# Hybrid streaming-encoder block: value, key and query columns regrouped into a 264-column and a 512-column projection

## Chip, cores and metric

The kernel runs on one core of one Trainium2 chip. The metric is device time in microseconds (us) of one execution; less is better. The kernel before has a median of 1688.1 us over three runs (1687.12 to 1690.24).

## What is computed

The reference is one layer on x of 1024 tokens by 1024 channels, with a memory of 256 tokens. Cut to what matters:

```python
h = _rmsnorm(x, norm_mix_g)
z = h @ w_in                       # one input projection, f32
hq, hf, hi, hg, fq, fk, fv, ff, mq, gate_logits = split(z)
y_a = _hgrn2_mixer(hq, hf, hi, hg, ...)              # gated linear recurrence
y_b = _fox_mixer(fq, fk, fv, ff, fox_f_bias, ...)    # forgetting attention
y_c = _memory_mixer(mq, rmsnorm(mem) @ mem_kv_w, ...)  # attention into 256 memory tokens
merged = sum(gate_i * (y_i @ w_br_i)); x = x + merged @ w_out
x = x + conv_glu_ffn(_rmsnorm(x, norm_ffn_g), ...)

# in _fox_mixer (8 heads of 64 channels):
log_f = log_sigmoid(f_logit + f_bias); Fc = cumsum(log_f)
s = q_norm . k_norm * scale + Fc[t] - Fc[s]; p = softmax(causal s); o = p @ v
```

The change concerns the projections of the forgetting attention (called fox in the code): `fv`, 512 value columns; `ff`, 8 forget logits, one per head; and `fk`, `fq`, keys and queries, of which the kernel projects one pair of heads (256 columns: 128 of keys, 128 of queries) before the attention begins.

## The kernel before

**Products.** Every f32 product is done as three matmuls of fp32r parts (`mm3`, L246 to L250): high by high (L248), high by low (L249), low by high (L250). The parts are made by `split` (L260): a cast to fp32r on ACT gives the high part (L254), a subtraction on DVE gives the low part (L262). K = 1024 is eight chunks of 128.

**Weights of this stage.** `weights` (L276) loads a piece of weights (two K-chunks of 512 columns or four of 256 or 264) with a DMA on SP's queue (L273) into `raw` (two buffers), and splits it into `wh` and `wl` (four buffers each, `WIDE`).

**The projection.** `token_major` (L793) loads all pieces of a block of columns and then goes over eight token blocks of 128: for each it takes a PSUM tile from `ps_proj` (named `pp` in the trace, three buffers), issues 8 x 3 = 24 matmuls with the normalised tokens (`uh`, `ul`, 128 x 128) as the stationary operand and the weights as the moving one, and calls `evac`, which copies the tile out and so frees its buffer for the block three later.

**The three passes.** `fox_values` (L823) calls it twice: value columns 0 to 255 (256 columns wide, evacuated by one ACT copy, L827), and value columns 256 to 511 with the 8 forget columns (264 wide, the ACT copy and a DVE operation, L829, that scales the forget logits and adds the bias `fbr` into `ffx`). Then come log-sigmoid and cumulative sum of the forget logits. `fox_proj` (L967) calls it for the first pair's keys and queries (256 wide, ACT copy into `z`, L973), and after every fourth block normalises z (L979 to L982).

**What is woven in.** `weave` (L98, called in L1331) alternates these projections with `memory` (cross-attention into the memory tokens): `mem_prep` loads one head's queries (`mqf`, L868), squares them on ACT (`msq`, L873), sums the squares with one-column matmuls on PE (L876) into a `tr` tile, and splits them into `mqh` and `mql`; `mem_parts` loads and splits the memory's keys and values (`mkv`, L858; `mkh` and `mvh` on POOL, the low parts on DVE); `mem_attn` does logits, softmax, transposes (L912) and the product with the values. The memory part is given a higher priority by `ahead`; a scheduler then turns the emitted program into one order of instructions per engine, and each engine runs its own order in sequence, waiting on semaphores. A wait thus holds back all that stands behind it on its engine.

**SP's queue at this place.** The bias `fbr` (4 KB, L818), the first `mqf` and the first `mkv` (512 KB each) are issued on SP one behind the other, between two weight loads.

**Afterwards** comes the attention proper with the second pair's projections, in an order set by a planner; its products of fox projections are recorded at L1229.

Of the kernel before, what the change touches and what calls it, by code (L numbers as in the profile page):

```python
# [197 lines left out]
def tile_block(ctx: ExitStack, tc: tile.TileContext, xT, memT, x_rows, mem_rows, vec, fbias, mats, hmask, w_first, w_cm, w_late, w_fqk, w_fv,  # L198
# [594 lines left out]
    def token_major(src, ncol, evac, lead=False):  # L793

        with tc.issue_after(late["load"].ins):
            per = 2 if ncol == HB else 4
            w = [weights(src[q], (per, ncol)) for q in range(KC // per)]
        if lead:
            yield
        for tb in range(8):  # L800
            ps = ps_proj()[:, :ncol]
            tsl = slice(tb * P, (tb + 1) * P)
            for k in range(KC):
                wh, wl = w[k // per]
                mm3(ps, uh[k][:, tsl], ul[k][:, tsl], wh[:, k % per, :], wl[:, k % per, :], k == 0, k == KC - 1)
            evac(tb, ps)
            yield
# [14 lines left out]
    negFd = tc.dram_tile([8, T], F32, name="negFd")  # L822

    def fox_values():
        for pc in range(2):
            def evac(tb, ps, pc=pc):
                S.activation(Vf[:, tb, pc * 256:(pc + 1) * 256], ps[:, :256], AF.Copy, scale=rt[:, tb:tb + 1])  # L827
                if pc:
                    V.scalar_tensor_tensor(out=ffx[:, tb, :], in0=ps[:, 256:264], scalar=rt[:, tb:tb + 1], in1=fbr,  # L829
                                           op0=ALU.mult, op1=ALU.add)  # L830
            yield from token_major(w_fv[pc], 264 if pc else 256, evac)

        S.activation(ffe, ffx, AF.Abs)
        S.activation(ffe, ffe, AF.Sigmoid)
        S.activation(ffe, ffe, AF.Ln)
        V.scalar_tensor_tensor(out=ffe, in0=ffx, scalar=0.0, in1=ffe, op0=ALU.min, op1=ALU.add)
        for n in range(2):
            pt = ps_tr()
            for b in range(4):
                PE.transpose(pt[:8, b * P:(b + 1) * P], ffe[:, 4 * n + b, :], ident)  # L840
            V.tensor_tensor_scan(negF[:, n * HB:(n + 1) * HB], ones[:8, 0:1].to_broadcast([8, HB]), pt[:8, :],
                                 0.0 if n == 0 else negF[:, HB - 1:HB], ALU.mult, ALU.subtract)
        SP.dma_start(negFd, negF)
        yield
# [79 lines left out]
    def memory():  # L924
        run_all(mem_prep(0))
        mem_parts()
        yield
        for h in range(4):
            if h < 3:
                run_all(mem_prep(h + 1))  # L930
            yield from mem_attn(h)
# [35 lines left out]
    def fox_proj():  # L967

        def evac(tb, ps):
            n, b = tb // 4, tb % 4  # L970
            if b == 0:
                fox_tile(0, n)
            S.activation(fox_z[0, n][:, b, :], ps, AF.Copy, scale=rt[:, tb:tb + 1])  # L973
            if b == 3:
                z = fox_z[0, n].rearrange("p b (h d) -> p (b h) d", d=64)
                r = cp.tile([P, 16], F32, tag="fr", name="fr", bufs=2)
                for i in range(2):
                    sq = gate_tile().rearrange("p (h d) -> p h d", d=64)
                    S.activation(sq, z[:, 8 * i:8 * i + 8, :], AF.Square)  # L979
                    V.reduce_sum(r[:, 8 * i:8 * i + 8], sq, axis=AX.X)  # L980
                rstd_small(r, r, 64)
                V.tensor_mul(z, z, r.unsqueeze(2).to_broadcast([P, 16, 64]))  # L982

        yield from token_major(w_fqk[0], 256, evac)

    qk, qk_ready, vh, vh_ready, nfs, nf_ready = {}, {}, {}, {}, {}, {}
    pt_ready, pt_free, rows_done, turn, kept = {}, {}, {-1: 0.0, -2: 0.0}, {}, {}
# [340 lines left out]
            yield "SP", 0.1, max(t, vh_ready[7])  # L1328
            SP.dma_start(Vf[:, tb, :], hid[tb])

    weave((chain(fox_values(), fox_proj()), 25), (ahead(memory(), AHEAD), 4 * MEM_STEPS))  # L1331
    parts[-1] = [(weights(w_fqk[1][q], (4, 256)), q, 0.0) for q in range(2)]
    pm.release()
    pf = pools["pf"] = Rounded(tc, name="pf", bufs=1, side="right", reuse_waits="tile")
    pf.small(("st", 4, 4))
# [760 lines left out]
def _layout(inp):  # L2096
    import numpy as np

    f = {k: np.asarray(v, dtype=np.float32) if np.asarray(v).dtype != np.float32 else np.asarray(v)
         for k, v in inp.items()}  # L2100
    c = np.ascontiguousarray

    def kmaj(a):

        return a.reshape(a.shape[0] // P, P, a.shape[1]).transpose(1, 0, 2)

    def chunks(a):

        k, n = a.shape
        return c(a.reshape(k // P, P, n // P, P).transpose(2, 1, 0, 3).reshape(n // P, P, k))  # L2110

    def cols(v):
        return v.reshape(-1, P).T

    x, mem = f["x"][0], f["mem"][0]
    w = f["w_in"][0]
    hq, hf, hi, hg, fq, fk, fv, ff, mq, gt = np.split(
        w, np.cumsum([512, 512, 512, 512, 512, 512, 512, 8, 512]), axis=1)
    o = {}
# [13 lines left out]
    o["fbias"] = c(np.broadcast_to(f["fox_f_bias"][0][None, :], (P, 8)))  # L2133
    i = np.arange(P)
    o["mats"] = c(np.concatenate([
        (i[:, None] == i[None, :]).astype(np.float32), np.ones((P, P), np.float32),
        np.where(i[:, None] >= i[None, :], 0.0, NEG).astype(np.float32),
        np.broadcast_to((np.arange(HB) % P != 0).astype(np.float32)[None, :], (P, HB))], axis=1))
    hm = []
    for H in (16, 8):  # L2140
        t = i.reshape(-1, 2, H)[:, 1, :].reshape(-1)
        hm.append(i[:, None] // H == (t // H - 1)[None, :])
    hm.append((i[:, None] // 8 == i[None, :] // 8) & (i[:, None] <= i[None, :]))
    o["hmask"] = c(np.concatenate(hm, axis=1).astype(np.float32))
    cm = np.concatenate([hq, hf, hg, mq, gt], axis=1)
    o["w_cm"] = chunks(cm)
    first = np.stack([o["w_cm"][16 + 8 * br + j].reshape(P, KC, P) for br, j in ORDER[:2]], axis=2)
    o["w_first"] = c(first.reshape(P, 2, 2 * KC * P // 2).transpose(1, 0, 2))

    def quartered(a):  # L2150

        q = kmaj(a).reshape(P, 2, 4, 2, P).transpose(0, 1, 3, 2, 4)
        return np.stack([q[:, h, c].reshape(P, -1) for h, c in ((0, 0), (0, 1), (1, 1), (1, 0))], axis=1)

    o["w_pair"] = c(np.stack([quartered(np.concatenate([cm[:, ch * P:(ch + 1) * P] for ch in pair], axis=1))
                              for pair in PAIRS]))

    def pieces(a, cuts):
        out = []
        for lo, hi_ in cuts:  # L2160
            p = kmaj(a[:, lo:hi_])
            out.append(np.stack([p[:, 0:4].reshape(P, -1), p[:, 4:8].reshape(P, -1)]))
        return out

    o["w_fqk"] = c(np.stack([pieces(np.concatenate([fk[:, p * P:(p + 1) * P], fq[:, p * P:(p + 1) * P]], axis=1),
                                    [(0, 256)])[0] for p in range(2)]))
    late = np.concatenate([m[:, p * P:(p + 1) * P] for p in (2, 3) for m in (fk, fq)], axis=1)
    o["w_late"] = c(np.stack([kmaj(m).reshape(P, 4, 2 * HB).transpose(1, 0, 2) for m in (late, hi)]))
    pv = pieces(np.concatenate([fv, ff], axis=1), [(0, 256), (256, 520)])
    o["w_fv0"], o["w_fv1"] = c(pv[0]), c(pv[1])  # L2170
    kv = f["mem_kv_w"][0]
    half = lambda m: kmaj(m).reshape(P, 4, 2 * HB).transpose(1, 0, 2)
    o["w_mkv"] = c(np.concatenate([half(kv[:, :512]), half(kv[:, 512:])]))
    o["w_br"] = c(np.stack([chunks(f[n][0]) for n in ("w_br_hgrn", "w_br_fox", "w_br_mem")]))
    o["w_out"] = chunks(f["w_out"][0])

    up = kmaj(f["ffn_w_up"][0]).reshape(P, 2, 4, 2, NF // 2, 2, P).transpose(4, 3, 0, 1, 5, 2, 6)
    up = np.stack([up[..., 0, 0, :, :], up[..., 0, 1, :, :], up[..., 1, 1, :, :], up[..., 1, 0, :, :]], axis=3)
    o["w_up"] = c(up.reshape(NF, P, 4, HB))

    wd = f["ffn_w_down"][0].reshape(NF // 2, 2, P, 2, HB).transpose(2, 3, 1, 0, 4)
    o["w_dn"] = c(wd.reshape(P, 4, NF // 2, HB))
    return o
# [19 lines left out]
```

## Time and profile before

| | us |
|---|---|
| Median of three runs (lowest, highest) | 1688.1 (1687.12, 1690.24) |
| The profiled execution's own time | 1688.31 |
| Its span, first to last instruction | 1686.5 |
| Around the span | 1.8 |
| TensorE (PE) busy | 1677.7 (99%), 8409 matmuls |
| VectorE (DVE), ScalarE (ACT), GpSimd (POOL) busy | 1170.4, 808.5, 326.6 |
| Mean granted TensorE clock | 1.000 of full speed |

All times of the trace are microseconds from the start of the span. A row of the timeline gives start, duration, engine, line, operation, output and inputs, the count, and in brackets how long the engine was idle before and what released it. "PEld" is the load of the stationary operand, which lies beside matmuls. The stage of the change begins at 258 us (first matmul of the first value block) and ends at 371 us (last block of the first pair's keys and queries). A matmul's own duration includes its way through the array (0.28 us at 256 columns), so what one costs in a stream is the distance between starts (0.12 us).

### The profile page before, as it was taken

The page shows a single profiled execution, that of the slowest core. Times are in us where ns is not written, and L with a number is a line of the kernel's source. Part 1 is how long each engine was busy: PE and PEld are TensorE (multiplying, and loading weights), DVE is VectorE, ACT ScalarE, POOL GpSimd, SP SyncE. Part 2 cuts the span into 40 slices and gives each one's busy share as a digit, 9 for nine tenths or more (in the row PEclk, how much of TensorE's full clock was granted, in tenths as well). Part 3 has the DMA queues.
Part 4 walks back from the last instruction along what each step waited for, and adds up shares of the span by engine and source line. Part 5 has one row for each costly group of instructions (what it writes and reads, how often), then busy time and mean ns, then how long its engine had stood idle before and what let it go on. Part 6 is the DMA issues. An engine that isn't in the chain of part 4 may idle for free.

```text
span 1686.5 us, 23254 instructions
## 1 busy us (share of the span) xinstructions
PE 1677.7 (99%) x8409; PEld 1415.8 (84%) x8409; DVE 1170.4 (69%) x2118; ACT 808.5 (48%) x1459; POOL 326.6 (19%) x430
## 2 busy tenths in 40 slices
PE   9999999999999999999999999999999999999999
PEld 7888889998888888888888888888888888888887
DVE  6966554558688766766856745988788888775664
ACT  6734444656576556666521333634344444533432
POOL 0200001336464423433201000211111111100000
PEclk9999999999999999999999999999999999999999
DMA  9442324122142233100337641666454454494782
GB/s 376 171 145 105 118 77 157 71 100 69 57 133 87 75 101 101 51 20 19 107 106 257 207 151 58 189 180 182 132 144 131 122 166 132 176 352 154 239 283 88
DMA packets 87348, 235.50 MB, mean 140 GB/s; under 512 B 9904, under 2 KB 12600, under 8 KB 87104
## 3 DMA queue, kind: packets, MB, share of 16 engines
q1 hardware_dynamic: 68032, 166.83, 28.4%
q0 software_dynamic: 18624, 66.59, 13.9%
q8 instruction: 66, 1.08, 0.3%
q10 hardware_dynamic: 576, 0.59, 0.1%
q14 instruction: 50, 0.41, 0.1%
HBM read 184.91 MB, written 72.13 MB: 152 GB/s over the span
## 4 chain that ended last, share of the span: by engine, by line
PE 96%; DVE 2%; ACT 1%; DMA 1%; issue 0%; ACTq 0%; DVEq 0%
PE pp L250 17%; PE pp L249 17%; PE pp L248 17%; PE pp L1229 10%; PE lg L248 5%; PE lg L250 5%; PE lg L249 5%; PE tr L250 3%; PE tr L249 3%; PE tr L248 3%; PE tr L1147 2%; PE po L1172 1%; PE lg L1085 1%; PE lg L1086 1%; PE po L248 1%; PE po L249 1%
## 5 line engine op out<-in xcount | busy, mean ns | idle before, releaser
L254 ACT CAST wh<-s 128x512 fp32r<-128x512 f32 x122 | 73.3, 620 | 133.1 <-PE pp L249 73.3
L254 ACT CAST wh<-rw 128x512 fp32r<-128x512 f32 x96 | 58.5, 619 | 113.8 <-PE pp L249 69.7
L254 ACT CAST wh<-raw 128x512 fp32r<-128x512 f32 (+2 forms) x85 | 63.9, 756 | 96.0 <-PE pp L249 76.3
L254 ACT CAST dwh<-wr 128x1024 fp32r<-128x1024 f32 (+1 forms) x41 | 40.2, 980 | 114.1 <-PE tr L249 37.6
L250 PE MATMUL pp<-uh,wl 128*128 128x512 f32 x224 | 89.0, 397 | 0.0
L248 PE MATMUL pp<-uh,wh 128*128 128x512 f32 x224 | 88.8, 396 | 0.0
L249 PE MATMUL pp<-ul,wh 128*128 128x512 f32 x224 | 88.4, 395 | 0.0
L1161 DVE TENSOR_TENSOR pl<-tr,ph 128x512 fp32r<-128x512 f32 (+1 forms) x96 | 51.4, 551 | 30.7 <-ACT ph L254 30.3
L1120 ACT ACTIVATE pt<-pt,st 128x128 f32<-128x128 f32 (+3 forms) x64 | 49.6, 775 | 45.9 <-DVE st L1116 30.6
L1229 PE MATMUL pp<-wl,uh 128*128 128x512 f32 (+1 forms) x192 | 70.0, 365 | 0.0
L1229 PE MATMUL pp<-wh,uh 128*128 128x512 f32 (+1 forms) x192 | 69.5, 362 | 0.0
L1229 PE MATMUL pp<-wh,ul 128*128 128x512 f32 (+1 forms) x192 | 69.4, 362 | 0.0
L262 DVE TENSOR_TENSOR dwl<-wr,dwh 128x1024 fp32r<-128x1024 f32 (+1 forms) x41 | 46.3, 1130 | 30.5 <-ACT dwh L254 30.5
L254 ACT CAST ph<-tr 128x512 fp32r<-128x512 f32 (+1 forms) x96 | 44.2, 477 | 41.0 <-PE tr L1147 39.6
L1124 POOL TENSOR_SCALAR pt<-pt,st 128x128 f32<-128x128 f32 (+3 forms) x64 | 52.0, 815 | 60.1 <-DVE st L1122 58.4
L1828 POOL DMA_DIRECT2D rw<-in_w_up x42 | 23.2, 558 | 200.0 <-DVE wl L1718 190.1
L1718 DVE TENSOR_TENSOR wl<-rw,wh 128x512 fp32r<-128x512 f32 x69 | 46.6, 687 | 21.2 <-PE pp L250 17.9
L1718 DVE TENSOR_TENSOR wl<-s,wh 128x512 fp32r<-128x512 f32 x85 | 57.9, 683 | 0.0
L262 DVE TENSOR_TENSOR wl<-raw,wh 128x512 fp32r<-128x512 f32 (+2 forms) x54 | 52.1, 964 | 7.0 <-ACT wh L254 7.0
L248 PE MATMUL pp<-wh,uh 128*128 128x256 f32 (+1 forms) x192 | 55.2, 287 | 0.0
L250 PE MATMUL pp<-wh,ul 128*128 128x256 f32 (+1 forms) x192 | 55.0, 286 | 0.0
L249 PE MATMUL pp<-wl,uh 128*128 128x256 f32 (+1 forms) x192 | 54.4, 283 | 0.0
(520 smaller groups left out, 5602.2 us busy)
## 6 DMA issues: line engine op xcount, KB each, us to landing
rw<-in_w_up POOLq DMA_DIRECT2D x42, 512.0 KB, 4.8
sd<-in_w_dn POOLq DMA_DIRECT2D x30, 512.0 KB, 6.0
br<-yd SPq DMA_DIRECT2D x30, 512.0 KB, 5.6
gd<-gt SPq DMA_DIRECT2D x48, 256.0 KB, 2.0
gt<-gd SPq DMA_DIRECT2D x48, 256.0 KB, 2.8
yd<-fc SPq DMA_DIRECT2D x44, 256.0 KB, 2.8
wr<-sd SPq DMA_DIRECT2D x20, 512.0 KB, 4.9
raw<-in_w_cm SPq DMA_DIRECT2D x18, 512.0 KB, 3.5
```

Source lines behind the costliest of these rows:

```text
L248: PE.matmul(ps, lh, rh, start=first, stop=False, skip_group_check=more)
L249: PE.matmul(ps, lh, rl, start=False, stop=False, skip_group_check=more)
L250: return PE.matmul(ps, ll, rh, start=False, stop=last, skip_group_check=more)
L254: return S.copy(out, in_)
L262: return (sub or V).tensor_sub(l, src, h.bitcast(F32))
L1120: S.activation(pt, pt, AF.Exp, bias=st[:, 2:3], accum_out=st[:, 3:4])
L1124: G.tensor_scalar(pt, pt, st[:, 3:4], 0.0, ALU.mult, ALU.add)
L1147: PE.transpose(ptr[:, j * P:(j + 1) * P], pts[j][:, sb * P:(sb + 1) * P], ident)
L1161: V.tensor_sub(pl[:, c], ptr[:, c], ph[:, c].bitcast(F32))
L1229: PE.matmul(o, a, b, start=q == i == 0, stop=q == KC - 1 and i == 2)
L1718: late["split"] = V.tensor_sub(l, src, h.bitcast(F32))
L1828: late["raw"] = (SP if begun else G).dma_start(raw[:, 2 * i:2 * i + 2, :], src[:, 2 * i:2 * i + 2, :])
```

## The change

The eight forget columns go with the first half of the values (one pass, 264 wide). The second half of the values and the first pair's keys and queries become one pass whose moving operand has 512 columns: per token block 24 matmuls of 512 columns in place of 48 of 264 and 256. Its weights come in four pieces of two K-chunks; since `wh` and `wl` have four buffers and the first pass holds two of them, the third piece gets tiles of its own (`xwh`, `xwl`). Each block of the wide pass has two ACT copies, one into `z` and one into the second half of the values. The number of steps that `weave` assumes for these projections goes from 25 to 17.

```diff
@@ token_major
         with tc.issue_after(late["load"].ins):
             per = 2 if ncol == HB else 4
-            w = [weights(src[q], (per, ncol)) for q in range(KC // per)]
+            own = [pm.tile([P, 4 * 264], F32R, tag=t, name=t) for t in ("xwh", "xwl")] if ncol == HB else None
+            w = [weights(src[q], (per, ncol), hl=own if q == 2 else None) for q in range(KC // per)]
@@ fox_values
-        for pc in range(2):
-            def evac(tb, ps, pc=pc):
-                S.activation(Vf[:, tb, pc * 256:(pc + 1) * 256], ps[:, :256], AF.Copy, scale=rt[:, tb:tb + 1])
-                if pc:
-                    V.scalar_tensor_tensor(out=ffx[:, tb, :], in0=ps[:, 256:264], scalar=rt[:, tb:tb + 1], in1=fbr,
-                                           op0=ALU.mult, op1=ALU.add)
-            yield from token_major(w_fv[pc], 264 if pc else 256, evac)
+        def evac(tb, ps):
+            S.activation(Vf[:, tb, :256], ps[:, :256], AF.Copy, scale=rt[:, tb:tb + 1])
+            V.scalar_tensor_tensor(out=ffx[:, tb, :], in0=ps[:, 256:264], scalar=rt[:, tb:tb + 1], in1=fbr,
+                                   op0=ALU.mult, op1=ALU.add)
+        yield from token_major(w_fv[0], 264, evac)
@@ fox_proj
-            S.activation(fox_z[0, n][:, b, :], ps, AF.Copy, scale=rt[:, tb:tb + 1])
+            S.activation(fox_z[0, n][:, b, :], ps[:, 256:], AF.Copy, scale=rt[:, tb:tb + 1])
+            S.activation(Vf[:, tb, 256:], ps[:, :256], AF.Copy, scale=rt[:, tb:tb + 1])
...
-        yield from token_major(w_fqk[0], 256, evac)
+        yield from token_major(w_fv[1], HB, evac)
@@ the stage
-    weave((chain(fox_values(), fox_proj()), 25), (ahead(memory(), AHEAD), 4 * MEM_STEPS))
-    parts[-1] = [(weights(w_fqk[1][q], (4, 256)), q, 0.0) for q in range(2)]
+    weave((chain(fox_values(), fox_proj()), 17), (ahead(memory(), AHEAD), 4 * MEM_STEPS))
+    parts[-1] = [(weights(w_fqk[q], (4, 256)), q, 0.0) for q in range(2)]
```

The rest of the diff packs the weights to match. Line numbers of the changed kernel are one higher than before from L798 to L823, one lower from L830 to L973 (the squares are L872, their sum L875), and the same after that; the bias operation is L828.

How instructions stand now: three places. The first is PE's order where the third token block of the first values ends and the fourth begins. Rows with `pp` are the projection's matmuls, `uh_93`, `ul_94` a block's last chunk, `uh_79` its first; a bracket names what the engine must wait for. Before:

```order
L248 MATMUL pp<-wh,uh_93 128x256
L249 MATMUL pp<-wl,uh_93 128x256
L250 MATMUL pp<-wh,ul_94 128x256
L248 MATMUL pp<-wh,uh_79 128x256 [waits DVE_49]
L249 MATMUL pp<-wl,uh_79 128x256
L250 MATMUL pp<-wh,ul_80 128x256
L248 MATMUL pp<-wh,uh_81 128x256
```

In the changed kernel, the same place:

```order
L248 MATMUL pp<-wh,uh_93 128x264
L249 MATMUL pp<-wl,uh_93 128x264
L250 MATMUL pp<-wh,ul_94 128x264
L875 MATMUL tr<-ones,msq_2294 128x1 [waits DMAHW6_49,Activation_49]
L875 MATMUL tr<-ones,msq_2294 128x1 x3
L248 MATMUL pp<-wh,uh_79 128x264 [waits DVE_49,PE_49]
L249 MATMUL pp<-wl,uh_79 128x264
L250 MATMUL pp<-wh,ul_80 128x264
```

The one-column matmuls on the first memory head's squares stand directly behind the third block now, and ahead of all of the fourth; before, they stood 41 matmuls further back, within the fifth block, where the rows read:

```order
L248 MATMUL pp<-wh,uh_89 128x256
L249 MATMUL pp<-wl,uh_89 128x256
L876 MATMUL tr<-ones,msq_2293 128x1 [waits DMAHW6_49,Activation_49]
L876 MATMUL tr<-ones,msq_2293 128x1 x3
L250 MATMUL pp<-wh,ul_90 128x256
```

The fourth block's first matmul takes the PSUM buffer of the first block, whose last reader is now a DVE instruction. The second place is DVE's order there, in the changed kernel (`mql`, `mkl` are the low parts of the memory's queries and keys):

```order
L766 SCALAR_TENSOR_TENSOR gt<-pp,rx 128x512 [waits DMAHW0_49,PE_49]
L262 TENSOR_TENSOR wl<-raw,wh 128x1024 [waits DMAHW7_49,Activation_49]
L262 TENSOR_TENSOR xwl<-raw,xwh 128x1024 [waits DMAHW2_49,Activation_49]
L828 SCALAR_TENSOR_TENSOR ffx<-pp,rt,fbr 128x8 [waits DMAHW0_49,Pool_49]
L828 SCALAR_TENSOR_TENSOR ffx<-pp,rt,fbr 128x8 [waits PE_49]
L262 TENSOR_TENSOR mql_2289<-mqf_2291,mqh_2288 128x1024 [waits DMAHW6_49,Activation_49]
L828 SCALAR_TENSOR_TENSOR ffx<-pp,rt,fbr 128x8 [waits PE_49]
L262 TENSOR_TENSOR mkl<-mkv_2313,mkh 128x1024 [waits DMAHW7_49,Pool_49]
```

The operations on the forget logits, of which the first waits for the DMA of the bias `fbr`, stand ahead of the memory's low parts; before, the first of them came in the second pass. On SP the loads of `mqf`, `mkv` and `fbr` keep their places behind one another. The third place is ACT's order, in the changed kernel:

```order
L827 ACTIVATE Vf<-pp,rt 128x256 [waits PE_49]
L254 CAST xwh<-raw 128x1024 [waits DMAHW2_49]
L827 ACTIVATE Vf<-pp,rt 128x256 [waits PE_49]
L872 ACTIVATE msq_2294<-mqf_2291 128x512 [waits DMAHW6_49]
L254 CAST mqh_2288<-mqf_2291 128x1024
L872 ACTIVATE msq_2300<-mqf_2291 128x512 [waits PE_49,Activation_49]
L254 CAST mqh_2321<-mqf_2324 128x1024 [waits DMAHW3_49]
L872 ACTIVATE msq_2327<-mqf_2324 128x512 [waits PE_49,Activation_49]
```

Before, the squares of the second head (`msq_2326` there) stood ahead of its cast; now the cast of 1024 columns stands ahead of them.

More of the change, by code (lines that the diff above doesn't have):

```diff
@@ L2163, in pieces @@
         return out
-    o["w_fqk"] = c(np.stack([pieces(np.concatenate([fk[:, p * P:(p + 1) * P], fq[:, p * P:(p + 1) * P]], axis=1),
-                                    [(0, 256)])[0] for p in range(2)]))
+    pair = [np.concatenate([fk[:, p * P:(p + 1) * P], fq[:, p * P:(p + 1) * P]], axis=1) for p in range(2)]
+    o["w_fqk"] = c(pieces(pair[1], [(0, 256)])[0])
+    wide = np.concatenate([fv[:, 256:], pair[0]], axis=1)
     late = np.concatenate([m[:, p * P:(p + 1) * P] for p in (2, 3) for m in (fk, fq)], axis=1)
     o["w_late"] = c(np.stack([kmaj(m).reshape(P, 4, 2 * HB).transpose(1, 0, 2) for m in (late, hi)]))
-    pv = pieces(np.concatenate([fv, ff], axis=1), [(0, 256), (256, 520)])
-    o["w_fv0"], o["w_fv1"] = c(pv[0]), c(pv[1])
+    o["w_fv0"] = c(pieces(np.concatenate([fv[:, :256], ff], axis=1), [(0, 264)])[0])
+    o["w_fv1"] = c(kmaj(wide).reshape(P, 4, 2 * HB).transpose(1, 0, 2))
     kv = f["mem_kv_w"][0]
```

## The prediction

> **What bounds the kernel now.** I read the page first: busy shares, the granted clock and the shares of the chain of waits.
>
> ```profile
> PE 1677.7 (99%) x8409; PEld 1415.8 (84%) x8409; DVE 1170.4 (69%) x2118; ACT 808.5 (48%) x1459; POOL 326.6 (19%) x430
> ...
> PEclk9999999999999999999999999999999999999999
> ...
> PE 96%; DVE 2%; ACT 1%; DMA 1%; issue 0%; ACTq 0%; DVEq 0%
> ```
>
> PE is busy for 99% of the span at the full granted clock, and it carries 96% of the chain that ends last. So the time is what PE has to do, plus what it waits. Next the stretches of the changed stage (columns: window, its length, busy PE, PEld, DVE, ACT, POOL, clock, DMA share, GB/s), and the complete list of PE's waits in the whole span.
>
> ```profile
> 256.00:300.00 44.00, 44.00 (x340) 42.58 (x339) 21.71 (x39) 21.57 (x43) 8.59 (x11) 1.00 0.46 156
> 300.00:341.00 41.00, 41.00 (x320) 39.52 (x319) 21.49 (x58) 25.18 (x64) 12.22 (x22) 1.00 0.14 53
> 341.00:371.00 30.00, 30.00 (x239) 28.88 (x238) 14.77 (x27) 17.60 (x37) 6.76 (x7) 1.00 0.15 55
> ```
>
> ```profile
> PE lg L248 <- ACT uh L437: 1.7, 1, 1.7
> PE tr L353 <- POOL dull L351: 1.0, 1, 1.0
> PE lg L1523 <- DVE X L1501: 0.7, 1, 0.7
> PE po L1172 <- DVE pl L1161: 0.5, 1, 0.5
> PE lg L1085 <- DVE st L1099: 0.4, 1, 0.4
> PE pp L250 <- DVE wl L1718: 0.4, 1, 0.4
> ```
>
> From 256 to 371 us PE is busy all the time, and none of its six waits has a line of this stage: memory's squares, softmax and loads lie entirely beside projections. A gain or loss of PE here therefore passes on to the end, since PE is as full in what follows. The change has two parts: cheaper matmuls, and a new order in which PE must wait.
>
> **Term 1: fewer, wider matmuls.** PE loses 192 matmuls: 384 of 256 columns and 192 of 264 become 192 of 264 and 192 of 512. The 264-wide ones keep their count; 384 of 256 turn into 192 of 512. What such matmuls cost in a stream, with the same operands (tokens stationary, weights moving), shows in the chain's rows of the second pair (256 columns, first row) and of the wide pass behind it (512 columns, the others):
>
> ```profile
> 372.58 9.48 PE pp L1229 x79
> ...
> 399.28 1.88 PE pp L1229 x8
> ...
> 402.86 2.52 PE pp L1229 x11
> ...
> 436.48 2.97 PE pp L1229 x13
> ...
> 466.20 2.73 PE pp L1229 x12
> ```
>
> At 256 columns 9.48 / 79 = 0.120 us each. At 512 columns 0.235, 0.229, 0.228 and 0.2275; the pieces are short and lie between others, so I take 0.230. A pair of 0.240 becomes 0.230: 192 x 0.010 = **1.9 us saved**, with 192 x 0.005 = 1.0 and 192 x 0.0125 = 2.4 as ends. The Trainium skill's page "TensorE: Matmul & The Clock Gate", section "Back-to-back issue gap", gives a warm gap of N/2.4 + 2.5 ns, that is a fixed part of 2.5 ns for each matmul; by it the saving would be about 192 x 2.5 ns = 0.5 us, an estimate from that page. The rows show more than that formula at either width, and a fixed part of about 10 ns, so the measurement decides.
>
> **Term 2: the wait at the fourth block.** In the order of before, PE goes from the third to the fourth value block without anything between, and the squares' one-column matmuls come 41 matmuls later. Now they stand between these blocks. The rows of before around that moment, of PE, SP, ACT, the landing times of the DMAs there (median us from issue to landing) and DVE:
>
> ```profile
> 272.27 0.28 PE L248 MATMUL pp<-wh,uh 128*128 128x256 f32 x1
> ...
> 277.19 0.95 PE L876 MATMUL tr<-ones,msq 128*128 128x1 f32 x8
> 278.01 0.36 PE L250 MATMUL pp<-wh,ul 128*128 128x256 f32 x1
> ```
>
> ```profile
> 269.50 0.33 SPq L273 DMA_DIRECT2D raw<-in_w_fqk  x1
> 269.88 0.45 SPq L868 DMA_DIRECT2D mqf<-mqd  x1
> 270.42 0.38 SPq L858 DMA_DIRECT2D mkv<-kvd  x1
> 270.99 0.33 SPq L818 DMA_DIRECT2D fbr<-in_fbias  x1
> ...
> 280.03 6.29 SPq L868 DMA_DIRECT2D mqf<-mqd  x2
> ```
>
> ```profile
> 272.48 0.47 ACT L827 ACTIVATE Vf<-pp,rt 128x256 f32<-128x256 f32 x1 [2.40 <-PE pp L250]
> 274.92 0.63 ACT L873 ACTIVATE msq<-mqf 128x512 f32<-128x512 f32 x1 [1.97 <-DMA mqf<-mqd]
> ...
> 284.94 0.64 ACT L873 ACTIVATE msq<-mqf 128x512 f32<-128x512 f32 x1 [5.34 <-DMA mqf<-mqd]
> 285.47 1.03 ACT L254 CAST mqh<-mqf 128x1024 fp32r<-128x1024 f32 x1
> ```
>
> ```profile
> mqf<-mqd SPq DMA_DIRECT2D x4, 512.0 KB, 3.3
> ...
> mkv<-kvd SPq DMA_DIRECT2D x2, 512.0 KB, 5.7
> ...
> fbr<-in_fbias SPq DMA_DIRECT2D x1, 4.0 KB, 5.3
> ```
>
> ```profile
> 276.52 1.92 DVE L262 TENSOR_TENSOR mql<-mqf,mqh 128x1024 fp32r<-128x1024 f32 x1 [7.05 <-ACT mqh L254]
> 278.37 1.21 DVE L262 TENSOR_TENSOR mkl<-mkv,mkh 128x1024 fp32r<-128x1024 f32 x1
> ...
> 298.97 0.23 DVE L829 SCALAR_TENSOR_TENSOR ffx<-pp,rt,fbr 128x8 f32<-128x8 f32 x1 [0.20 <-ACT Vf L827]
> ```
>
> The fourth block starts at 272.27 here; in the change the first three blocks are 264 wide, 72 matmuls that come 72 x 8/256 x 0.120 = 0.1 to 0.3 us later, say 272.4 (this returns in the second pass, whose columns fall by as many). The squares cannot be ready then: ACT waited 1.97 us for `mqf` and began at 274.92, because the load was issued at 269.88, behind a weight load. That load stands at the same place of SP's order and is bound by the same DVE subtraction, so nothing makes it earlier. Squares end at 274.92 + 0.63 = 275.55. **PE waits 275.55 - 272.4 = 3.1 us** (3.0 to 3.3). Behind it are the whole fourth block and all that follows on PE.
>
> The eight one-column rows take 0.82 us (277.19 to 278.01), to 276.4. Then the fourth block needs the PSUM buffer of the first, and its last reader is now the bias operation on DVE, which needs `fbr`. That tiny load is last of the four on SP: 270.99 + 5.3 = 276.3. With 0.2 us of DVE work (row 298.97) and a handover, the buffer is free at about 276.6: **0.2 us more** (0 to 0.4). Before, `fbr` had 28 us of slack, its first reader coming at 298.97. First place: 3.3 us, 3.0 to 3.7. Nothing on ACT or DVE hurries this; both are idle, waiting for the same loads.
>
> **Term 3: the second head's squares.** Its `mqf` takes the buffer that `mkl` reads. From the freed bias operation at 276.6, `mql` (1.92) and `mkl` (1.21) and a bias operation of 0.2 end at 279.9, so the load is issued at about 280.0 as before (280.03), and lands after 3.3 us (the median) to 4.9 us (284.94 - 280.03): 283.3 to 284.9, I take 284.0. ACT now does the cast first (1.03, of which a little overlaps with what follows) and then the squares (0.64): ready at 284.8 to 286.5, middle 285.5. PE, from 276.6, has 57 matmuls of about 0.121 and eight one-column ones: 6.9 + 0.8, so it arrives at 284.3. **Wait 1.2 us**, 0.5 to 2.2. This is a wait that the first one itself did not absorb, since the loads are tied to DVE, which was held back by the same `fbr`.
>
> **Term 4: the first softmax.** The transposes of `mpt` now stand in the middle of the second memory logits, each behind POOL's scaling (L905 before). No row shows them there; the only wait of PE for POOL in the profile is 1.0 us (`dull`), before none occurs here. So 0 to 1.0, and I take 0.4, nearer to none because memory's whole chain is late together with PE.
>
> Other edits cost nothing: a second ACT copy per wide block has cover, since ACT is busy 17.60 of 30 us in the last window; without that cover each would cost its 0.47 us, eight times 3.8 us. The 512-wide tile is freed one copy later, with three buffers and a block of 24 x 0.230 = 5.5 us in between. The weights are loaded, cast and subtracted in six pieces of up to 1056 columns as before, by DMAs of the same size.
>
> **Sum.** Waits 3.3 + 1.2 + 0.4 = 4.9 us (3.5 to 6.9); less 1.9 (1.0 to 2.4): +3.0, between +1.1 and +5.9. Against the profiled execution's own 1688.31 us (span 1686.5 and 1.8 around it; the median of the runs is 1688.1, 0.2 lower) this gives **1691.3 us**, 1689.4 to 1694.2.
>
> **Rivals.** (A) *No wait: the change pays.* If `mqf` and `fbr` land before PE needs them, only term 1 remains: 1688.3 - 1.9 = 1686.4 (1685.9 to 1687.3), not slower. Its point is 272.4 us for `mqf` and its squares, thus a landing 3.1 us earlier, and 275.3 for `fbr`. For it: a 512 KB load can take 3.3 us instead of 5.0. Against it: even then 269.88 + 3.3 + 0.63 = 273.8 is 1.4 us too late, and before's ACT row shows the wait. 10%.
>
> (B) *The clock falls.* Between 272.4 and 276.6 PE would do eight one-column matmuls in 4.2 us; no such gap exists now, the longest is 1.7 us, and the grant is 1.00 in every window. If the grant halves for as long as the pause lasts, 3.4 us of PE's time does 1.7 us of work: +1.7; for twice that, +3.4. So 1693.0 to 1694.7. The Trainium skill, "TensorE: Matmul & The Clock Gate", table in Part 1, says that after an idle window of about 3.4 us the clock goes to half; no run here shows it. Against it: the window must fall inside the pause, and one-column matmuls interrupt it. 15%.
>
> (C) *Wider is not cheaper.* If 512 columns cost twice 0.120, term 1 is gone: 1688.3 + 4.9 = 1693.2. The rows at 0.2275 to 0.235 speak against it. 5%.
>
> **How the numbers follow.** The forecast has 70%, A 10%, B 15%, C 5%. The range 1686.2 to 1695.0 takes in A and most of B. A measurement can tell about 0.2% from no change, 3.4 us: slower means above 1691.5, faster below 1684.7. The forecast's own spread lies about that upper line: of its 70%, 33 above and 37 below; B and nearly all of C above, A within. Slower 0.52, same 0.45, faster 0.03.
>
> **What would show it.** In the new profile the list of PE's waits should hold `tr L875 <- ACT msq L872` with about 3 us the longest, perhaps one more of the same line near 1, and a `pp` of the stage waiting for DVE `ffx` with some tenths; PE's busy time should be about 1676, 1.9 us less. The wide pass should run at 0.230 us a matmul. I am wrong if PE's list has no row of L875, if the 512-column matmuls stream at 0.240, or if windows behind 272 us show a clock under 1.00.

## The result, and the profile after

| | before | changed |
|---|---|---|
| median of ten runs each (lowest to highest), us | 1688.38 (1687.11 to 1690.24) | 1693.26 (1691.15 to 1694.91) |
| ratio, 95% interval | | 1.0028 (1.0020 to 1.0036) |
| the profiled execution's own time, span, us | 1688.31, 1686.5 | 1691.90, 1690.1 |
| matmuls | 8409 | 8217 |

The change makes the kernel slower by 4.9 us at the median, 0.28%. The page's busy row and PE's complete list of waits in the changed kernel (us in total, times, longest):

```profile
PE 1678.1 (99%) x8217; PEld 1407.9 (83%) x8217; DVE 1170.4 (69%) x2118; ACT 806.6 (48%) x1459; POOL 328.0 (19%) x430
```

```profile
PE tr L875 <- ACT msq L872: 2.5, 1, 2.5
PE lg L248 <- ACT uh L437: 1.6, 1, 1.6
PE tr L353 <- POOL dull L351: 1.0, 1, 1.0
PE lg L1085 <- DVE st L1099: 1.0, 1, 1.0
PE lg L1523 <- DVE X L1501: 0.7, 1, 0.7
PE po L1172 <- DVE pl L1161: 0.5, 1, 0.5
PE pp L248 <- DVE ffx L828: 0.4, 1, 0.4
PE pp L250 <- DVE wl L1718: 0.4, 1, 0.4
```

The two new rows are the predicted ones: squares 2.5 us, bias operation 0.4. A third, L1085, stands at another place than before: the 1.0 us is at 401 us, among the attention's first logits, where before has no wait; before's 0.4 on that line is at 504 us. PE did 192 matmuls fewer and yet was busy 0.4 us longer. The rows around the gap, of PE, ACT, DVE and SP, show the wait, and the windows (busy PE, PEld, DVE, ACT, POOL, then the granted clock) why busy time did not fall:

```profile
273.60 0.28 PE L250 MATMUL pp<-wh,ul 128*128 128x264 f32 x1
276.38 1.05 PE L875 MATMUL tr<-ones,msq 128*128 128x1 f32 x8 [2.49 <-ACT msq L872]
277.84 0.56 PE L248 MATMUL pp<-wh,uh 128*128 128x264 f32 x1 [0.41 <-DVE ffx L828]
278.20 0.42 PE L249 MATMUL pp<-wl,uh 128*128 128x264 f32 x1
278.42 0.42 PE L250 MATMUL pp<-wh,ul 128*128 128x264 f32 x1
...
280.62 0.39 PE L248 MATMUL pp<-wh,uh 128*128 128x264 f32 x1
280.84 0.29 PE L249 MATMUL pp<-wl,uh 128*128 128x264 f32 x1
```

```profile
275.69 0.63 ACT L872 ACTIVATE msq<-mqf 128x512 f32<-128x512 f32 x1 [1.30 <-DMA mqf<-mqd]
```

```profile
277.47 0.36 DVE L828 SCALAR_TENSOR_TENSOR ffx<-pp,rt,fbr 128x8 f32<-128x8 f32 x2 [3.79 <-DMA fbr<-in_fbias]
```

```profile
271.33 0.32 SPq L867 DMA_DIRECT2D mqf<-mqd  x1
271.70 0.42 SPq L857 DMA_DIRECT2D mkv<-kvd  x1
272.23 0.38 SPq L819 DMA_DIRECT2D fbr<-in_fbias  x1
```

```profile
274.00:276.00 2.00, 0.00 (x0) 0.00 (x0) 0.00 (x0) 0.70 (x2) 0.00 (x0) 1.00 1.00 352
276.00:278.00 2.00, 1.21 (x9) 1.16 (x10) 0.53 (x3) 1.73 (x3) 0.62 (x1) 0.86 0.90 348
278.00:280.00 2.00, 2.00 (x10) 2.00 (x11) 2.00 (x3) 0.16 (x1) 0.43 (x1) 0.50 0.05 12
280.00:282.00 2.00, 2.00 (x15) 2.00 (x15) 0.76 (x1) 0.00 (x0) 0.00 (x0) 0.79 0.60 203
```

From 278.20 to 280.84 matmuls start 0.22 us apart, then 0.12. The granted clock fell to half at the end of the gap. Twelve matmuls at 0.22 instead of 0.121, and a first one at 0.36, cost 1.4 us.

**Where the difference of these two executions sits.** The stage's first matmul, a piece of the chain in the attention (402.86 in the chain of before) and the last matmul give three marks. First before, then changed:

```profile
258.16 0.28 PE L248 MATMUL pp<-wh,uh 128*128 128x256 f32 x1
...
1682.47 0.39 PE L250 MATMUL po<-dbh,dwl 128*128 128x512 f32 x1
```

```profile
259.56 0.28 PE L248 MATMUL pp<-wh,uh 128*128 128x264 f32 x1
...
1686.09 0.39 PE L250 MATMUL po<-dbh,dwl 128*128 128x512 f32 x1
```

```profile
408.00 2.52 PE pp L1229 x11
```

The changed kernel is 1.4 us late before the stage begins, 5.1 at the second mark and 3.6 at the end. The first 1.4 us have nothing to do with the change: its execution had the clock at half near the start as well, before's had not (windows of the changed kernel; before shows 1.00 there):

```profile
8.00:10.00 2.00, 2.00 (x6) 1.57 (x5) 2.00 (x5) 2.00 (x4) 0.00 (x0) 0.50 1.03 406
10.00:12.00 2.00, 2.00 (x7) 1.57 (x7) 1.48 (x3) 1.09 (x3) 0.00 (x0) 0.70 1.03 420
```

So between the first two marks the change costs 3.7 us: waits 2.5 + 0.4 + 1.0, clock 1.4, less the saving of about 2.0; 0.4 is left to small gaps. From 372 us of before on, PE's order is the same in both kernels, so the distance can be read row by row: 4.0 us there, 5.1 from the wait on L1085 on, and 3.5 at 514 us. The 1.6 us come back between 504 and 514 us, where it is before that loses them: a load of weights took 6.3 us to land there (3.3 in the changed kernel, 4.4 in before with 12 warm-up products, e8 below), and ACT, which feeds that place, waited for it:

```profile
501.60 0.62 ACT L254 CAST wh<-raw 128x512 fp32r<-128x512 f32 x1 [3.00 <-DMA raw<-in_w_late]
```

Without the start's 1.4 us the changed kernel is 2.6 us late at 372 us and 2.2 at the end.

### The profile page after: what moved, and what is told of

Its sections match the earlier page's. It is cut to its first block, busy times and chain, and to the rows that moved or that the text cites. A ratio compares the mean times of both kernels' runs of the same rounds, so it can differ in the third digit from the quotient of the medians.

```text
span 1690.1 us, 22873 instructions
## 1 busy us (share of the span) xinstructions
PE 1678.1 (99%) x8217; PEld 1407.9 (83%) x8217; DVE 1170.4 (69%) x2118; ACT 806.6 (48%) x1459; POOL 328.0 (19%) x430
## 4 chain that ended last, share of the span: by engine, by line
PE 95%; DVE 2%; DMA 1%; ACT 1%; issue 0%; POOL 0%; SPq 0%; ACTq 0%; DVEq 0%
PE pp L248 17%; PE pp L249 17%; PE pp L250 17%; PE pp L1229 9%; PE lg L248 5%; PE lg L250 5%; PE lg L249 5%; PE tr L249 3%; PE tr L250 3%; PE tr L248 3%; PE tr L1147 2%; PE po L1172 1%; PE lg L1085 1%; PE lg L1086 1%; PE po L1171 1%; PE po L249 1%
## 5 line engine op out<-in xcount | busy, mean ns | idle before, releaser
L1124 POOL TENSOR_SCALAR pt<-pt,st 128x128 f32<-128x128 f32 (+3 forms) x64 | 52.0, 816 | 58.5 <-DVE st L1122 56.7
L249 PE MATMUL pp<-yl,wh 128*128 128x512 f32 x128 | 50.1, 392 | 0.0
L248 PE MATMUL pp<-yh,wh 128*128 128x512 f32 x128 | 50.1, 396 | 0.0
L248 PE MATMUL pp<-T2h,wh 128*128 128x512 f32 x128 | 50.0, 391 | 0.0
```

The lines of the kernel that those rows point to most:

```text
L248: PE.matmul(ps, lh, rh, start=first, stop=False, skip_group_check=more)
L249: PE.matmul(ps, lh, rl, start=False, stop=False, skip_group_check=more)
L1124: G.tensor_scalar(pt, pt, st[:, 3:4], 0.0, ALU.mult, ALU.add)
```

## The experiments

All times are medians; ratios are against the kernel before on the same chip. Twelve runs.

| run | us | ratio (95%) |
|---|---|---|
| e1 forget columns with the first half, no wide pass | 1695.19 | 1.0037 (1.0025 to 1.0050) |
| e2 wide pass alone | 1690.82 | 1.0011 (1.0002 to 1.0020) |
| e3 changed, gap filled | 1692.05 | 1.0024 (1.0015 to 1.0033) |
| e4 changed, first mqf and bias on POOL's queue | 1695.39 | 1.0040 (1.0027 to 1.0053) |
| e5 changed, bias added late | 1696.33 | 1.0042 (1.0030 to 1.0055) |
| e6 changed, first mqf on POOL's queue | 1692.12 | 1.0015 (1.0006 to 1.0023) |
| e7 changed, 12 warm-up products | 1692.06 | 1.0016 (1.0007 to 1.0025) |
| e8 before, 12 warm-up products | 1687.23 | 0.9990 (0.9981 to 0.9999) |
| e9 changed, bias loaded first, 12 products | 1712.29 | 1.0136 (1.0119 to 1.0153) |
| e10 as e9, memory's pace 40 | 1710.53 | 1.0128 (1.0113 to 1.0143) |
| e11 as e9, no address moved | 1691.42 | 1.0018 (1.0009 to 1.0027) |
| e12 as e11, memory's pace 40 | 1689.88 | 1.0007 (0.9998 to 1.0016) |

My theory (W): the loss is the wait for squares and bias, and the clock that falls in it. The rival (O): the loss sits in the wide pass or behind it. The first four runs separate them.

**e1, one half of the change.** The passes stay three; only the forget columns move:

```diff
-                if pc:
+                if not pc:
...
-            yield from token_major(w_fv[pc], 264 if pc else 256, evac)
+            yield from token_major(w_fv[pc], 256 if pc else 264, evac)
...
```

> The kernel before with one part of the change alone: the eight forget columns go with the first half of the values (264 columns, then 256, then 256); no wide operand. The squares' one-column matmuls stand directly behind the third block, as in the changed kernel. Theory W (the loss is the wait for squares and bias behind the third block and the clock that falls in it): slower than the changed kernel by the saving of about 2 us that it lacks, 1694 to 1697, with a wait of about 2.5 us on L876 and a clock under 1.00 in the window 256 to 300. Rival O (the loss sits in the 512-wide pass or in what comes behind it): about as before, 1688.4, no wait on L876.

Measured 1695.19, with these rows (waits; window):

```profile
PE tr L876 <- ACT msq L873: 2.8, 1, 2.8
```

```profile
256.00:300.00 44.00, 41.18 (x291) 39.64 (x290) 21.25 (x45) 19.55 (x40) 8.35 (x11) 0.92 0.39 131
```

As W said: moving eight columns, without any wide operand, costs at least as much as the whole change. In this trace the clock fell for twice as long (0.92 over 44 us is 7 us at half; 0.96 in the changed kernel is 3.5), so its distance from the changed kernel is not the missing saving alone. The first logits near 400 us do not wait here; the 0.6 on L1085 is at 510 us, where before has its 0.4. The 1.0 at 401 us came only with the wide pass.

**e2, the other half.** First pass 256 wide, then the wide pass. It leaves out the product of the forget columns; the eight bias operations come behind the pass and read value columns instead:

```diff
-            V.scalar_tensor_tensor(out=ffx[:, tb, :], in0=ps[:, 256:264], ...)
-        yield from token_major(w_fv[0], 264, evac)
+        yield from token_major(w_fv[0], 256, evac)
+        for tb in range(8):
+            V.scalar_tensor_tensor(out=ffx[:, tb, :], in0=Vf[:, tb, :8], ...)
...
```

> The other part alone: first values 256 columns, then the 512-wide pass as in the changed kernel. It leaves out the product of the forget columns: the forget logits are made from eight value columns instead, in eight DVE operations behind the first pass. The squares stand within the fifth block, as before. Theory W: 1688.4 minus the saving of 192 x 0.010 to 0.013 us = 1685.9 to 1686.6, no wait of PE on the squares, clock 1.00 from 256 to 300. Rival O: about 1693.

Measured 1690.82: 2 us slower than before where W wanted about 2 faster. The clock is 1.00 from 256 to 300 and no wait is left on squares, but new ones appear (lines are one higher in this kernel):

```profile
PE lg L1086 <- DVE st L1100: 1.4, 2, 1.3
...
PE po L248 <- ACT mph L254: 0.6, 1, 0.6
...
PE lg L248 <- ACT mpt L901: 0.3, 1, 0.3
```

So W was not the whole: the wide pass saves PE time and PE then waits elsewhere, for memory's softmax and for the attention's first. Rival O was right that something sits behind the stage. Not all of the traced execution's 2.5 us is that: 1.6 lie at the start, where its 512-wide matmuls stand 0.43 us apart until 10.4 us and before's 0.23. Counted from there it is 0.5 us late at 372 us, 1.9 behind the wait on the first logits and 0.7 at the end, and the saving of 2 is gone even so.

**e3, the gap filled.** 24 matmuls that nothing uses, into the squares' tile, ahead of them; the first head's squares are placed by hand behind them, and the steps of `weave` become 18 and 7 more for memory:

```diff
+        prs0.append(ps_tr())
+        for i in range(24):
+            PE.matmul(prs0[0][:, :256], uh[i % 8][:, :P], wh[:, 0, :256], start=True, stop=True)
...
```

> The changed kernel with 24 further matmuls of 256 columns (2.9 us) that write the squares' PSUM tile ahead of them: 8 ahead of the third block, 16 between it and the squares. Their result is overwritten and used by nothing. They put work where PE stood idle. If the clock's fall costs time by itself: clock 1.00 from 256 to 300, no L875 wait, and 1.4 to 2 us less than the changed kernel, 1691 to 1692. If only the wait counts and the clock costs nothing: 1693 to 1694, the same as the changed kernel, or up to 0.5 us more where the filler is longer than the wait.

Measured 1692.05, 1.2 us under the changed kernel's median, with the clock at 1.00 from 256 to 300, 0.3 us of waiting left on the squares and 1.3 on the first logits. That is the upper edge of what was expected if the clock's fall costs time by itself. But the intervals of the two ratios overlap (1.0015 to 1.0033 here, 1.0020 to 1.0036 for the changed kernel), so the medians do not show it; the trace's 12 slow matmuls do.

**e4, loads on another queue.**

```diff
-    SP.dma_start(fbr, fbias)
+    G.dma_start(fbr, fbias)
...
-        SP.dma_start(t, mqd[h])
+        (G if h == 0 else SP).dma_start(t, mqd[h])
```

> The changed kernel, with the first memory head's load (mqf) and the bias (fbr) issued on POOL's queue instead of SP's, where they stood behind weight loads. PE's order is kept: squares directly behind the third block. Theory W, if the loads are issued some 5 us earlier there: waits and the clock's fall go, 1685.9 to 1686.6, faster than before. If they are not earlier, since the place in memory is not free before: as the changed kernel, 1693. Rival O: 1693 though the waits are gone.

Measured 1695.39, no faster than the changed kernel. The loads were early (squares began without waiting for a DMA), but DVE's order had changed (waits of PE, then DVE's rows):

```profile
PE pp L248 <- DVE ffx L828: 3.0, 1, 3.0
...
PE tr L875 <- ACT msq L872: 1.1, 1, 1.1
```

```profile
277.85 1.22 DVE L262 TENSOR_TENSOR mkl<-mkv,mkh 128x1024 fp32r<-128x1024 f32 x1 [3.81 <-POOL mkh L258]
278.99 0.48 DVE L828 SCALAR_TENSOR_TENSOR ffx<-pp,rt,fbr 128x8 f32<-128x8 f32 x3
```

The bias operation now stands behind `mkl`, which waits for memory's keys. The data of `ffx` was there; its engine was not. What holds PE is not the load alone but a PSUM buffer whose last reader is in DVE's queue.

**e5, no DVE reader of PSUM.** ACT copies the forget logits, one DVE addition follows the pass:

```diff
+            S.activation(ffx[:, tb, :], ps[:, 256:264], AF.Copy, scale=rt[:, tb:tb + 1])
+        yield from token_major(w_fv[0], 264, evac)
+        V.tensor_add(ffx, ffx, fbr.unsqueeze(1).to_broadcast([P, 8, 8]))
```

> The changed kernel with the forget logits copied out of PSUM by ACT (eight more small copies, scaled by rt) and the bias added once for all blocks behind the pass, so that no DVE operation and no load of the bias holds a PSUM buffer. The squares then stand within the fifth block again. Theory W: no wait of PE on squares or bias, clock 1.00 from 256 to 300, and counted from the first hundred matmuls on 2 to 5 us less than the changed kernel; in time 1686.5 to 1690, the lower end if memory's later softmax finds as much cover as before, the upper end if its waits appear as in the run with the wide pass alone. Rival O (the loss sits behind the stage): 1692 or more.

Measured 1696.33: a miss by 6 us, and in the range of rival O. The squares are back in the fifth block, so without the DVE reader they are not pulled forward. But then:

```profile
PE tr L911 <- POOL mpt L904: 3.4, 1, 3.4
```

```profile
365.44 2.90 POOL L267 TENSOR_TENSOR fr<-fr,mhalf 128x16 f32<-128x16 f32 x1 [8.12 <-DVE fr L266]
368.32 3.83 POOL L904 TENSOR_SCALAR mpt<-mpt,mst 128x256 f32<-128x256 f32 x6
```

POOL has the 2.9 us power of the keys' and queries' norm ahead of memory's last softmax, and PE has nothing left to do meanwhile; behind this wait the clock fell again (0.94 from 371 to 420 us). Adding up PE's order with each matmul at its distance between starts gives what cover is left (an estimate, in us of PE's own work from the stage's first matmul on; what counts is how far the last two columns lie apart):

| | first squares | last transposes of memory | last projection |
|---|---|---|---|
| before | 19.0 | 104.8 | 111.2 |
| changed | 14.2 | 103.5 | 107.5 |
| e2 | 18.9 | 108.3 | 105.0 |
| e5 | 18.8 | 108.3 | 102.3 |
| e6 | 19.2 | 108.2 | 105.5 |
| e11 | 18.8 | 108.6 | 105.2 |
| e12 | 18.8 | 106.7 | 107.5 |

Before, 6 us of projections lie behind memory's last transposes; in the changed kernel 4 are left. Where the squares stand late (e2, e5, e6, e11), PE's order has memory's last transposes 3.5 us further back, and none are left. Theory T from here on: the early squares come from the bias; with late squares the shorter projections no longer cover memory's last softmax.

**e6, only the squares' load moved.**

```diff
-        SP.dma_start(t, mqd[h])
+        (G if h == 0 else SP).dma_start(t, mqd[h])
```

> The changed kernel with only the first memory head's load moved to POOL's queue; the bias stays on SP's, behind a weight load, and on DVE as the last reader of the PSUM buffer. The squares stand late again (within the fifth block). If two waits lie one behind the other, taking away the first leaves the second: PE waits 2 to 3.5 us for the bias operation ahead of the fourth block instead of 2.5 for the squares, and the time stays at 1692 to 1694. If the squares' wait alone was the loss: 1688 to 1690.

Measured 1692.12, where the chain of two waits was to give 1692 to 1694; before is 0.8 us slower on this chip than beside the changed kernel, so by the ratio it is 2.2 us faster than the changed kernel. The first wait is gone and the second takes its place, smaller than expected (1.3, not 2 to 3.5): the bias, now directly behind the weight load, was issued at 271.17 and its operation began at 274.74, 3.6 us later, where the changed kernel took 5.2 (272.23 to 277.47):

```profile
275.11 0.36 PE L248 MATMUL pp<-wh,uh 128*128 128x264 f32 x1 [1.27 <-DVE ffx L828]
```

The clock stays at 1.00 behind this gap of 1.3 us. The squares went late here although the bias's reader is still on DVE, so the bias is not the only thing that decides their place; what else does was not tried.

**e7 and e8, the start.** Both kernels with more warm-up products, which PE does while it waits for the first tokens:

```diff
-NDULL = 8
+NDULL = 12
```

> The changed kernel with 12 instead of 8 warm-up products at the start, so that PE has work for nearly all of the time in which it waits for the first tokens (1.6 us). If the fall of the clock at 8 us that its profile shows comes from that wait and happens in many of its runs: no window under 1.00 in the first 20 us, 1 to 1.5 us less, 1691.8 to 1692.3. If it is chance in one run: 1693.3.

> The kernel before with the same 12 warm-up products. If the fall at the start happens in part of its runs only: 0 to 1 us less than before and a narrower spread, 1687.5 to 1688.8. The difference between this pair of kernels then is what the change costs without the start: 2 to 4 us.

Measured 1692.06 and 1687.23. In neither trace does the clock fall in the first 20 us, and the spreads shrink from 3.8 to 2.4 us and from 3.1 to 1.3. But the pair differs by 4.8 us, as the first pair did, where 2 to 4 were expected: the start explains much of the spread, not the difference. In e7 the squares wait 2.9 us and the clock from 256 to 300 is 0.96. On the first logits it waits 0.15 us, as e8 does; its other new wait is 1.2 us on POOL at 645 us (`tr L1147 <- POOL pt L1124`).

**e9 and e10, the bias loaded first.**

```diff
-    SP.dma_start(fbr, fbias)
...
+    cv = cp.tile([P, NCV], F32, tag="cv", name="cv"); fbr = cp.tile([P, 8], F32, tag="fbr", name="fbr")
...
+    S.dma_start(cv, vec); S.dma_start(fbr, fbias)
...
```

> The changed kernel with the 32 bytes per partition of the bias loaded at the very start, on ACT's queue, into a tile of its own, and with 12 warm-up products; nothing else is edited. The squares go back into the fifth block by themselves. Theory T (the early squares came from the bias; and since projections have 2.2 us less work, memory's last softmax no longer finds cover): no wait on squares or bias, clock 1.00 from 256 to 300, but 1 to 5 us of waits on mpt, mph or mpl between 345 and 372, where last transposes stand 3 us behind the last projection matmul instead of 6 ahead of it; 1687 to 1691. Rival (only bias and squares cost): 1685 to 1685.8, that is 1687.2 of the kernel before with 12 products less 1.5 to 2.2.

> The same, with the number of steps that the weaving assumes for memory raised from 28 to 40, by which projections end behind memory's last transposes again (by 0.8 us of matmuls; 6.4 before, 4.0 in the changed kernel). Theory T: the waits between 345 and 372 shrink to under 1 us, 1685 to 1687, and faster than the kernel before with 12 products (1687.2). Rival (the pace does not matter, since each softmax step has its own delay): as the run with the bias first, within 0.5 us.

Measured 1712.29 and 1710.53, 20 us and more over everything expected. No wait explains it: PE was busy, with fewer matmuls in the same time. The new 32-byte tile had moved every later tile of its side by 32 bytes. e11 and e12 put the bias into an unused filler tile instead (e12 raises memory's steps to 40 as e10 does):

```diff
+    fbr = top.tile([P, 8], F32, tag="fbr", name="fbr"); top.tile([P, 48], F32, tag="fill", name="fill_top")
```

> The run with the bias first again, instruction for instruction in the same order, but with the bias in a part of an unused filler tile, so that no other tile's address moves by 32 bytes. If the 17 us that the run with the bias first lost behind 793 us come from that shift (its 512-wide matmuls took 231 to 236 ns there against 227 in the kernel before with 12 products): they take 227 again and the time is 1687 to 1690. If they come from the early load: 1712. Within the stage, theory T: waits of 1 to 2 us between 345 and 372 on memory's last softmax, 1 to 1.5 us for the first softmax of the attention (L1085), none on squares or bias; thus 0.5 to 2 us slower than the kernel before with 12 products (1687.2).

> The same with the step count of memory at 40. Theory T: under 1 us of waits within the stage, the saving of about 2 us kept there, and 1 to 1.5 us of it given back in the wait on L1085: 1685.5 to 1687.5, within 0.1% of the kernel before with 12 products. If the saving reaches the end whole: 1685.0 to 1685.4.

Measured 1691.42 and 1689.88. The same window of e9, then of e11:

```profile
1400.00:1600.00 200.00, 200.00 (x862) 161.44 (x861) 138.22 (x170) 79.62 (x103) 13.83 (x24) 1.00 0.60 202
```

```profile
1400.00:1600.00 200.00, 200.00 (x884) 165.60 (x883) 135.69 (x164) 81.47 (x102) 11.30 (x20) 1.00 0.62 209
```

200 us hold 862 matmuls or 884: 0.232 or 0.226 each. PE's order is the same row for row; only addresses differ. For the stage itself e11 and e12 bear T out. e11 has no wait on squares or bias, the clock is 1.00 there, and it pays on memory's last softmax (0.6 and 0.2) and on L1085 (1.3). Its time misses the expected 1687 to 1690 by 1.4 us: in its trace the clock fell at the start in spite of the 12 products (0.90 and 0.93 in the first two 10 us), and PE waits 1.3 us at 908 us (L1659), which no theory named. In e12, with projections ending behind memory again, the waits on memory's last softmax are gone, one of 0.6 on an earlier softmax (293 us) has come, and L1085 stays:

```profile
PE lg L1085 <- DVE st L1099: 1.4, 2, 1.3
...
PE lg L248 <- ACT mpt L900: 0.6, 1, 0.6
```

e12 takes 3.4 us less than the changed kernel and cannot be told from before (1.0007, 0.9998 to 1.0016), but it needs 12 products, with which before takes 1687.23; its expectation of 1685.5 to 1687.5 was missed by 2.4. About one of that lies at the start, where PE waits 1.2 us for the first tokens (L437) and no such wait is listed in e8; the bias's DMA, which stands ahead of weight loads on ACT's queue, is the likely reason. Within the stage e12 gains 1.3 us on e8, and at the first logits it gives 1.7 back. No version beat e8.

## Why the prediction was right, and where its steps failed

The time was forecast as 1691.3 and came at 1693.26, inside the range, slower as the larger chance said. One of the prediction's own signs of being wrong came true: the windows behind 272 us show a clock under 1.00. The stage itself cost about what the sum said, +3.0: at 372 us, counted from the stage's start, the changed kernel is 2.6 us late, and e7 2.9 behind e8. That the sum fits is partly luck, as its terms show.

- **What bounds the kernel:** held. PE stayed at 99%, and what it waited in this stage was found again at the second mark.
- **Term 1, the saving.** In the traces the mean distance between starts, from one such matmul to the next, is 0.1217 us for the 256-wide ones of before's passes (359 pairs) and 0.2329 for the 512-wide ones of the wide pass (168): 192 x (0.2434 - 0.2329) = 2.0 us, forecast 1.9. The fixed part of some 10 ns stands; a saving of only 0.5 us does not.
- **Term 2, squares and bias.** The mechanism was right, at its place and with its names. Forecast 3.1 + 0.2, measured 2.49 + 0.41; 2.9 + 0.4 in e7. It is smaller here since PE came 1.4 us later (the start's clock) and the load only 0.8. (The bias's slack before was 22.7 us from its landing at 276.29; the 28 count from its issue. Nothing hangs on it.)
- **Term 3, the second head's squares:** forecast 1.2, measured nothing. PE came late by the clock's fall itself, just as the squares were ready. The step that reckoned PE's arrival at 284.3 took a full clock behind the gap; the squares were ready at 287.06 and PE began them at 287.11.
- **Term 4:** forecast 0.4 for `mpt`, none measured in the changed kernel.
- **Rival B was given 15% and happened** in both traces of the changed order (windows 0.50 behind the gap; e7 0.96 over 44 us), at 1.4 us where 1.7 was its lower end. It should have been the forecast: 1691.3 less terms 3 and 4 (1.6), plus 1.7, would have been 1691.4 with the right parts. As it is, the sum came close by luck, with two terms that were not there (1.6 us) in place of one that was (1.4).
- **What was missing:** the sum treated the 1.9 us saved as reaching the end, and everything behind the stage as unchanged. In e2, e3, e6, e11 and e12 PE waits 1.2 to 1.3 us at the attention's first logits, L1085 (L1086 in e2, L1102 in e3), in the changed kernel 1.0; in e7 0.15. In the changed kernel the chain of waits there begins with memory's last write (L920), behind which SP issues the second pair's weights, and then runs over ACT, DVE and POOL:

```profile
377.55 0.32 SPq L920
...
379.43 6.97 DMA raw<-in_w_late
...
395.25 3.29 POOL fr L956
398.53 1.42 POOL pt L1124
399.95 0.43 POOL nfm L1074
...
400.40 0.29 DVE pt L1099
...
400.85 0.47 PE lg L1085
```

The same write and load in before:

```profile
371.32 0.32 SPq L921 DMA_DIRECT2D ycld<-ycl  x1
...
373.32 0.90 SPq L1207 DMA_DIRECT2D raw<-in_w_late  x2
```

Memory ends behind the projections now: its last product is at 375.76 and the last projection's at 372.96, where before had 369.53 and 370.47. So the load goes out 6.1 us later while PE comes 4.0 later, and 2.1 us of slack are gone. POOL's power for the norm of keys and queries, its softmax step and its mask then set when the first logits can go on. The sentence of the prediction that failed is: "A gain or loss of PE here therefore passes on to the end". In e1 a loss did; in e12 a gain of 1.3 us ended at the chain that PE had been covering, and in the changed kernel the chain itself came later. I had looked only for waits that existed before, of which this stage had none, and not for how little slack stood behind them.
- **Rival A** (the change pays if loads are early) is refuted beyond its condition: e11 and e12 have no wait on squares or bias left, which is what early loads were to bring, and do not pay. **Rival C** is refuted by term 1.

**What stays open.** The traced executions differ by 3.6 us in the first pair, of which 1.4 are the start's clock, and by 3.4 in e7 against e8; the medians differ by 4.9 and 4.8. So 1.3 and 1.4 us of the medians' differences are in neither pair of traces. Of e7's runs four have a mean clock of 0.999 and average 1691.4, six 0.998 and average 1692.2 (one at 0.997 took 1691.4), so a longer fall of the clock in runs without a trace would explain some 0.9; that is a loose correlation, and its cause was not tried. The waits behind the stage also differ between traces of the same kernel (L1085 1.0 in the first, 0.15 in e7, which waits 1.2 at 645 us instead), and why was not tried.

## What to carry to other kernels

Before you save time on a full engine, ask for each place where it waits for nothing how much slack the others have there: a stage with no waits may be one that is just covered, and what you take from the cover can return as waits, as it did in e12. An operation added to the release of a PSUM buffer brings its engine's whole queue, and every load that it reads, into the path of the matmuls three blocks later; here eight columns did that. And when a small tile is added, keep the addresses of the others.

## What the runs showed of the hardware

- A gap in PE's work of 2.5 us, with 1 us of one-column matmuls and 0.4 us more of waiting behind it, halved the granted clock for 3.4 us (the windows' 0.86, 0.50 and 0.79; matmuls lost 1.4 us in it); in e1, where the wait was 2.8, the mean from 256 to 300 us was 0.92. A gap of 1.3 us (e6) did not. At the start, a wait of 1.6 us behind small products did so in the changed kernel's trace and one of 1.7 did not in before's, so length alone does not decide it. The Trainium skill, "TensorE: Matmul & The Clock Gate", table in Part 1, speaks of a whole idle window of about 3.4 us; the gap here was shorter as pure idleness, and the rows show the fall anyway. From the end of the third block (273.88) to the fourth's first matmul (277.84) it is 4.0 us; whether the one-column matmuls in between count was not tried.
- Moving tiles by 32 bytes made the matmuls of the same program (from 1400 to 1600 us, all 512 wide) take 0.232 us instead of 0.226 (e9 against e11); the medians lie 20.9 us apart. Which operand's address does it was not tried.
- A 4 KB load took 5.1 us from issue to landing behind three loads of 512 KB on the same queue (5.3 in before), and 1.8 us on POOL's queue (e4).
